# A running sum as one scan instruction, and half of a product moved from GpSimd to VectorE, in a two-layer hybrid decoder

## The chip, the cores and the metric

The kernel runs on one core of a Trainium2 chip. The metric is the device time of one execution in microseconds (us). A run with a profile is one execution on the chip with the hardware profiler on; it has its own time, and the span that its records cover is a little shorter. The engines are PE (TensorE), DVE (VectorE), ACT (ScalarE), POOL (GpSimd) and SP, which only issues DMAs here. Each engine takes its instructions in the order in which the program lists them for that engine.

## The reference

Two decoder layers on 256 positions of width 2048 in float32. In each layer one input projection gives the columns of three token mixers: a gated short convolution, a latent attention of 8 heads, and an RWKV-7 time mixing of 8 heads of 64. Their gated outputs are joined, projected and normed into the residual stream. The change lies in the RWKV branch:

```python
w = -jax.nn.softplus(-(w0 + jnp.tanh(wd) @ w2)) - 0.5
decay = jnp.exp(-jnp.exp(w.astype(jnp.float32)))
a = jax.nn.sigmoid(a0 + ad @ a2)
kk = kk / jnp.maximum(jnp.linalg.norm(kk, axis=-1, keepdims=True), 1e-12)
k = k * (1 + (a - 1) * k_a)
...
def step(state, inp):
    r_t, w_t, k_t, v_t, a_t, b_t = inp          # a_t = -kk, b_t = kk * a
    sa = jnp.einsum('bhvk,bhk->bhv', state, a_t)
    state = (state * w_t[:, :, None, :] + sa[..., None] * b_t[:, :, None, :]
             + v_t[..., None] * k_t[:, :, None, :])
    return state, jnp.einsum('bhvk,bhk->bhv', state, r_t)
...
y = (yf - ym) * lax.rsqrt(yv + RWKV_GN_EPS)     # per head, over 64 channels
```

`decay` is exp(-c * sigmoid(...)) with a constant c, so a product of decays over positions is the exponential of a running sum of sigmoids.

## The kernel before, in words

Channels lie on the 128 partitions and positions along the free axis, so a group of 512 columns is four blocks `b` of 128 channels x 256 positions. Each float32 matmul is three passes (`mm3`, lines 338 to 340): weights and activations are split into a high part `hi_...` (a cast by ACT) and a low rest `lo_...` (a subtraction by DVE), and high x high, high x low and low x high are added in PSUM. A weight tile of two rows of 128 gives a block of 24 matmuls of 128x256; a group of columns has eight such blocks, named here k0+0, k0+2, k4+0 and so on to k12+2.

The order of the work. Each layer goes through the groups k, r, a, v, cq, cc, ch, cb, cg of the input projection (`in_group`), then the key/value projection of the attention (`mla_kv`: four pairs of tiles `pkn` and `pvt`), its query projection (`mla_q`: four of `pqn` and `pqp`), the late groups rg, mg0, mg1, and the output projection. The three mixers are Python generators. After each block of matmuls a `tick` lets every generator run up to its next `yield`, so a yield sets between which blocks a generator's instructions are emitted: one yield fewer, and all that follows in that generator is emitted one tick sooner. A scheduler then merges what was emitted into the order of each engine, with raised priority for weight splits (`split_w`) and for evictions of PSUM.

The RWKV generator (`rwkv`) runs these steps, which the prediction names by their tiles:

- `rwkv_decay`: two low-rank matmuls per block; ACT's Tanh makes the decay's input (`cuma`) and the input of a (`tha`). Six shifted additions on DVE, between the two padded buffers `cuma` and `cumb`, make the running sum within each chunk of 64 positions, with a yield after each. ACT's exponentials of it are `pe` (with minus) and `pinv` (with plus).
- `rwkv_scale`: `kp` is the scaled key, `kkn` the normed key. The tile `bk` holds, for 16 pairs of block and chunk, 64 columns of one of them and 64 of the other, each times `pinv`. Even heads lie on the partitions 0 to 63 and odd heads on 64 to 127; for the odd heads the two are in the other order. The even heads' two products are DVE's, 64 partitions x 1024 each; the odd heads' are POOL's, one per chunk (`chunk`, line 575), eight of 64x256. `ar` holds `kkn` and the receptance times `pe`, eight DVE instructions of 128x256.
- `rwkv_products`: PE's pair products `pg` of `bk` with `ar`, per chunk (line 624).
- `rwkv_inverse`, `rwkv_pairs`: the inverse of a triangular matrix in each chunk, transposes, and products with the values.
- `rwkv_chain`: for the four chunks one after the other, PE's `prh` (state times ar, line 797), DVE's `rhs`, PE's `pu` (line 804), its copies to `uvt` by DVE and ACT, PE's state update `pst` (line 820), and the new state `st` by DVE. After every second chunk PE makes the outputs `py` (lines 773 and 782), and ACT copies them to `y`.
- `rwkv_norm`: the group norm of `y`. DVE's sum `gm`, its scaling, `y` minus `gm`; ACT's square `gsq`; DVE's sum `gv`, an inverse root by twelve small instructions on 128x16 (`grs`, `nr_g`), `y` times `grs`; then PE's transposes `pt` (line 863) and ACT's `yy` from them.
- `rwkv_gate`, after the group rg.

Of the kernel before, what the change touches and what calls it, by code (L numbers as in the profile page):

```python
# [13 lines left out]
AF = mybir.ActivationFunctionType  # L14
ALU = mybir.AluOpType
AX = mybir.AxisListType

P = 128
# [18 lines left out]
KAPPA = float(math.exp(-0.5))  # L37
# [73 lines left out]
def hybrid_layers(ctx: ExitStack, tc: tile.TileContext, x, positions, xT, w_in, w_out, w_uq, w_ukv, par, wa_in, gb_in,  # L111
# [32 lines left out]
    V, A, G, T = Gated(nc.vector, "V"), Gated(nc.scalar, "A"), nc.gpsimd, nc.tensor  # L144

    def after(inst, earlier):

        tc.add_manual_dep(inst.ins, earlier.ins.name,
                          mybir.DependencyInfo(mybir.DependencyClass.NoSync, mybir.DependencyReason.DATA),
                          reason="loads no earlier than needed")  # L150
# [28 lines left out]
    def zeros(rows):  # L179

        return cs[rows, K_CM + P:K_CM + 2 * P].unsqueeze(1).to_broadcast([64, 2, P])
# [3 lines left out]
    def slot(tag, name, shape=(P, 4, S), bufs=1, dt=F32):  # L185
        return sl.tile(list(shape), dt, tag=tag, name=name, bufs=bufs)

    def s4(name, shape=(P, 4, S), dt=F32):
        return slot("s4", name, shape, N4, dt)

    def c4(name, shape=(P, 4, S), dt=F32):
        return slot("c4", name, shape, NC4, dt)

    def s8(name, shape=(P, 8, S), dt=F32):
        return slot("s8", name, shape, N8, dt)
# [154 lines left out]
    def plan():  # L350

        for l in range(L):
            for names in (MAIN, None, LATE):
                if names is None:
                    yield from ((f"ukv{l}_{i}", 0, 2, w_ukv[l, i]) for i in range(4))
                    yield from ((f"uq{l}_{i}", 0, 4, w_uq[l, i]) for i in range(4))
                for name in names or ():
                    first = l == 0 and name == GROUPS[0]
                    for k0, nk in STEPS if first else [(k, 4) for k in (0, 4, 8, 12)]:
                        yield f"{name}{l}", k0, nk, w_in[l, GROUPS.index(name)]  # L360
            for g in range(3):
                yield from ((f"wo{l}_{g}", k0, 4, w_out[l, g]) for k0 in ORDER)
            for i in range(2):
                yield from ((f"wo{l}_3_{i}", k0, 4, w_out[l, 3][:, :, i * 256:i * 256 + 256]) for k0 in ORDER)

    loads, ready, asked = plan(), {}, []
# [62 lines left out]
    def shift_mix(pq, dst, u, mcol):  # L429

        col = pq["col"]
        with tc.high_priority(AHEAD):
            A.activation(dst, u, AF.Identity, scale=col(mcol + pq["om"]))
            V.scalar_tensor_tensor(dst[:, 1:S], u[:, 0:S - 1], col(mcol), dst[:, 1:S], ALU.mult, ALU.add)
# [66 lines left out]
    def rwkv_decay(l, pq, st, us):  # L501
        col = pq["col"]
        wa, ws = c4(f"wa{l}", (P, 2, 512)), c4(f"was{l}", (P, 2, 512), F32R)
        for r in halves:
            after(nc.gpsimd.dma_start(wa[r], wa_in[l].rearrange("(q r) c -> r q c", q=2)), loaded[0])
        A.copy(ws, wa)
        for i in range(2):
            r = halves[1 - i]
            V.tensor_tensor(ws[r, i, :], wa[r, i, :], ws[r, i, :].bitcast(F32), ALU.subtract)
        zl = c4(f"wal{l}", (P, 2, S), F32R)  # L510
        for i, r in enumerate(halves):
            G.tensor_copy(zl[halves[1 - i], i, :].rearrange("p (j c) -> p j c", c=P), zeros(halves[1 - i]))
        wa_x = sm.tile([P, S], F32, tag="rs", name=f"wax{l}", bufs=2)
        shift_mix(pq, wa_x, us, Q_MUWA)
        A.activation(wa_x[0:64, :], wa_x[0:64, :], AF.Tanh)
        cuma = s8(f"cuma{l}", (P, 4, 4, 96))
        cumb = s8(f"cumb{l}", (P, 4, 4, 96))
        V.memset(cuma[:, :, :, 0:32], 0.0)
        V.memset(cumb[:, :, :, 0:32], 0.0)
        tha = s4(f"tha{l}")  # L520
        xh = sm.tile([P, 2, S], F32R, tag="b2", name=f"wah{l}", bufs=3)
        for i, r in enumerate(halves):
            for o in halves:
                A.copy(xh[o, i, :], wa_x[r, :])
            V.tensor_tensor(zl[r, i, :], wa_x[r, :], xh[r, i, :].bitcast(F32), ALU.subtract)

        def lora(o, i, b):
            c = slice(b * P, b * P + P)
            T.matmul(o, ws[:, i, c], xh[:, i, :], start=True, stop=False)
            T.matmul(o, ws[:, i, c], zl[:, i, :], start=False, stop=True)  # L530

        yield
        for b in range(4):
            pw = pm.tile([P, S], F32, tag="m", name=f"pw{l}_{b}")
            lora(pw, 0, b)
            A.activation(cuma[:, b, :, 32:96], pw.rearrange("p (c t) -> p c t", c=4), AF.Tanh,
                         scale=0.5, bias=col(pq["hw"] + b))
            pa = pm.tile([P, S], F32, tag="m", name=f"pa{l}_{b}")
            lora(pa, 1, b)
            A.activation(tha[:, b, :], pa, AF.Tanh, scale=0.5, bias=col(pq["ha"] + b))  # L540
            if b % 2:
                yield
        ca = cuma.rearrange("p b c t -> p (b c) t")
        cb = cumb.rearrange("p b c t -> p (b c) t")
        V.tensor_scalar(ca[:, :, 32:96], ca[:, :, 32:96], 0.5, 0.5, ALU.mult, ALU.add)
        for d in (1, 2, 4, 8, 16, 32):
            V.tensor_tensor(cb[:, :, 32:96], ca[:, :, 32:96], ca[:, :, 32 - d:96 - d], ALU.add)
            ca, cb = cb, ca
            yield
        pe = slot("pe", f"pe{l}", (P, 16, 65))  # L550
        V.memset(pe[:, :, 0:1], 1.0)
        A.activation(pe[:, :, 1:65], ca[:, :, 32:96], AF.Exp, scale=-KAPPA)
        pinv = s4(f"pinv{l}")
        A.activation(pinv.rearrange("p b (c t) -> p (b c) t", t=64), ca[:, :, 32:96], AF.Exp, scale=KAPPA)
        st.update(pe=pe, pinv=pinv, tha=tha)
        yield

    def rwkv_scale(l, pq, st):
        col = pq["col"]
        kx, kkn, rx, tha, pe, pinv = (st[k] for k in ("kx", "kkn", "rx", "tha", "pe", "pinv"))  # L560
        kp = s4(f"kp{l}")
        for b in range(4):
            A.activation(kp[:, b, :], tha[:, b, :], AF.Identity, scale=col(pq["hk"] + b), bias=col(pq["ok"] + b))
        V.tensor_tensor(kp, kp, kx, ALU.mult)
        V.tensor_scalar(tha, tha, 0.5, 0.5, ALU.mult, ALU.add)
        yield
        bk = s8(f"bk{l}", (P, 16, P))
        ar = s8(f"ar{l}", (P, 4, 2, S))
        c16 = lambda a: a.rearrange("p b (c t) -> p (b c) t", t=64)
        lo_, hi_ = halves  # L570
        bkc = bk.rearrange("p (b c) t -> p b c t", c=4)

        def chunk(c, src, at):
            cc = slice(c * 64, c * 64 + 64)
            return G.tensor_tensor(bkc[hi_, :, c, at:at + 64], src[hi_, :, cc], pinv[hi_, :, cc], ALU.mult)

        for c in range(3):
            chunk(c, kp, 0)
        for b in range(4):
            V.scalar_tensor_tensor(chunks(ar[:, b, 0, :]), chunks(kkn[:, b, :]), -1.0,  # L580
                                   pe[:, b * 4:(b + 1) * 4, 0:64], ALU.mult, ALU.mult)
            if b % 2:
                yield
        V.tensor_tensor(kkn, kkn, tha, ALU.mult)
        ready_ = []
        for c in range(4):
            if c == 2:
                chunk(3, kp, 0)
            ready_.append([chunk(c, kkn, 64)])
        yield  # L590
        V.tensor_tensor(bk[lo_, :, 0:64], c16(kkn)[lo_], c16(pinv)[lo_], ALU.mult)
        V.tensor_tensor(bk[lo_, :, 64:128], c16(kp)[lo_], c16(pinv)[lo_], ALU.mult)
        yield
        for b in range(4):
            v = V.tensor_tensor(chunks(ar[:, b, 1, :]), chunks(rx[:, b, :]), pe[:, b * 4:(b + 1) * 4, 1:65], ALU.mult)
        yield
        st["ar"], st["bk"], st["kp"], st["ready"] = ar, bk, kp, [r + [v] for r in ready_]

    def rwkv_v(l, pq, st, uv):
        rx = st["rx"]  # L600
# [734 lines left out]
    for l in range(L):  # L1335
        u, t = {}, {}
# [47 lines left out]
```

## Time and profile before

| | us |
|---|---|
| time of the kernel before, median of 3 runs | 924.45 |
| lowest and highest of them | 924.32, 926.1 |
| the profiled execution | 928.7 |
| span of its records | 926.9 |
| mean granted clock of PE in it | 0.993 |

How to read the rows below. A row of the timeline has the start in us, the duration in us (for several instructions in one row, up to the end of the last), engine, line, operation, what is written `<-` what is read, shapes, and the count. In square brackets stands how long the engine had been idle before it and what ended that. A helper records every operation of DVE and ACT, so their line is L137 throughout and the tile's name tells them apart. A row of the waits has the engine that waited, what it was to do, whose work it waited for, and then the sum, the count and the longest wait in us. A row of the windows has the stretch, its length, the busy time of PE, PE's weight loads, DVE, ACT and POOL with their counts, then the granted clock of PE (1.00 is full), the share of the DMA engines' time and GB/s. A row of the groups has the busy time in us and the mean of one instruction in ns, then the idle time before. A row of the chain has the start, what the piece adds to the chain, and the instruction.

### The profile page before, as it was taken

The page shows a single profiled execution, that of the slowest core. Times are in us where ns is not written, and L with a number is a line of the kernel's source. Part 1 is how long each engine was busy: PE and PEld are TensorE (multiplying, and loading weights), DVE is VectorE, ACT ScalarE, POOL GpSimd, SP SyncE. Part 2 cuts the span into 40 slices and gives each one's busy share as a digit, 9 for nine tenths or more (in the row PEclk, how much of TensorE's full clock was granted, in tenths as well). Part 3 has the DMA queues.
Part 4 walks back from the last instruction along what each step waited for, and adds up shares of the span by engine and source line. Part 5 has one row for each costly group of instructions (what it writes and reads, how often), then busy time and mean ns, then how long its engine had stood idle before and what let it go on. Part 6 is the DMA issues. An engine that isn't in the chain of part 4 may idle for free.

```text
span 926.9 us, 18425 instructions
## 1 busy us (share of the span) xinstructions
PE 909.6 (98%) x7719; PEld 868.5 (94%) x7719; DVE 680.2 (73%) x1132; ACT 466.1 (50%) x716; POOL 44.9 (5%) x59
## 2 busy tenths in 40 slices
PE   8999999999999999999999999999999999999996
PEld 7999999999899999889899999899998999998895
DVE  6687899886479885666767688688865898755665
ACT  5756536443465775434346465364434657654430
POOL 0210120000000000000010003200000000000000
PEclk9999999999999999999999999899999999999998
DMA  8965355354426526955564554354544354359542
GB/s 291 297 197 182 137 189 164 138 183 137 160 96 224 175 99 193 359 177 171 193 211 177 183 182 154 128 180 137 183 139 141 134 204 164 97 182 367 176 135 91
DMA packets 47523, 165.12 MB, mean 178 GB/s; under 512 B 13446, under 2 KB 22198, under 8 KB 32582
## 3 DMA queue, kind: packets, MB, share of 16 engines
q1 hardware_dynamic: 39680, 150.35, 47.4%
q10 hardware_dynamic: 5072, 9.57, 3.4%
q0 software_dynamic: 2688, 4.03, 1.6%
q8 instruction: 60, 0.98, 0.4%
q14 instruction: 23, 0.19, 0.1%
HBM read 158.61 MB, written 5.32 MB: 177 GB/s over the span
## 4 chain that ended last, share of the span: by engine, by line
PE 93%; DVE 3%; DMA 2%; ACT 1%; POOL 1%; SPq 0%; issue 0%; DVEq 0%; ACTq 0%
PE po L338 6%; PE po L340 6%; PE po L339 6%; PE u_mg L340 3%; PE u_mg L338 3%; PE u_mg L339 3%; PE u_ch L338 2%; PE u_cc L338 2%; PE u_cg L340 2%; PE u_cg L339 2%; PE u_cg L338 2%; PE u_rg L340 2%; PE u_cb L340 2%; PE u_cb L339 2%; PE u_cb L338 2%; PE u_a L340 2%
## 5 line engine op out<-in xcount | busy, mean ns | idle before, releaser
L137 DVE TENSOR_TENSOR lo_wo<-w_wo,hi_wo 128x1024 fp32r<-128x1024 f32 x57 | 69.4, 1223 | 51.6 <-ACT hi_wo L137 50.1
L137 ACT CAST hi_wo<-w_wo 128x1024 fp32r<-128x1024 f32 x57 | 59.8, 1053 | 80.8 <-PE po L340 55.7
L338 PE MATMUL u_mg<-x,hi_mg 128*128 128x256 f32 x256 | 72.6, 283 | 0.0
L340 PE MATMUL u_mg<-x,lo_mg 128*128 128x256 f32 x256 | 72.6, 283 | 0.0
L339 PE MATMUL u_mg<-x,hi_mg 128*128 128x256 f32 x256 | 72.6, 283 | 0.0
L137 DVE TENSOR_TENSOR lo_mg<-w_mg,hi_mg 128x1024 fp32r<-128x1024 f32 x32 | 39.0, 1222 | 19.0 <-ACT hi_mg L137 18.9
L340 PEld LDWEIGHTS u_mg<-x,lo_mg 128*128 128x128 f32 x256 | 49.1, 192 | 0.0
L339 PEld LDWEIGHTS u_mg<-x,hi_mg 128*128 128x128 f32 x256 | 49.1, 192 | 0.0
L338 PEld LDWEIGHTS u_mg<-x,hi_mg 128*128 128x128 f32 x256 | 49.0, 192 | 0.0
L137 ACT CAST hi_mg<-w_mg 128x1024 fp32r<-128x1024 f32 x32 | 33.6, 1049 | 25.9 <-PE u_mg L339 18.5
L339 PE MATMUL po<-lo_wo,ma 128*128 128x512 f32 (+1 forms) x128 | 46.4, 362 | 0.0
L340 PE MATMUL po<-hi_wo,ma 128*128 128x512 f32 (+1 forms) x128 | 46.4, 362 | 0.0
L338 PE MATMUL po<-hi_wo,ma 128*128 128x512 f32 (+1 forms) x128 | 45.8, 363 | 0.0
L338 PE MATMUL u_cq<-x,hi_cq 128*128 128x256 f32 x128 | 37.7, 294 | 0.0
L338 PE MATMUL u_k<-x,hi_k 128*128 128x256 f32 x128 | 36.4, 289 | 1.2 <-ACT hi_k L137 1.2
L339 PE MATMUL u_cq<-x,hi_cq 128*128 128x256 f32 x128 | 37.1, 290 | 0.0
L340 PE MATMUL u_cq<-x,lo_cq 128*128 128x256 f32 x128 | 37.1, 290 | 0.0
L338 PE MATMUL u_ch<-x,hi_ch 128*128 128x256 f32 x128 | 37.0, 289 | 0.0
L338 PE MATMUL u_cc<-x,hi_cc 128*128 128x256 f32 x128 | 36.7, 289 | 0.0
L340 PE MATMUL u_cg<-x,lo_cg 128*128 128x256 f32 x128 | 36.6, 286 | 0.0
L338 PE MATMUL u_cg<-x,hi_cg 128*128 128x256 f32 x128 | 36.4, 284 | 0.0
L339 PE MATMUL u_cg<-x,hi_cg 128*128 128x256 f32 x128 | 36.4, 284 | 0.0
(424 smaller groups left out, 3418.4 us busy)
## 6 DMA issues: line engine op xcount, KB each, us to landing
w_wo<-in_w_out_dram SPq DMA_DIRECT2D x24, 1024.0 KB, 6.2
w_mg<-in_w_in_dram SPq DMA_DIRECT2D x16, 1024.0 KB, 4.9
w_r<-in_w_in_dram SPq DMA_DIRECT2D x8, 1024.0 KB, 5.8
w_a<-in_w_in_dram SPq DMA_DIRECT2D x8, 1024.0 KB, 4.8
w_v<-in_w_in_dram SPq DMA_DIRECT2D x8, 1024.0 KB, 4.8
w_cq<-in_w_in_dram SPq DMA_DIRECT2D x8, 1024.0 KB, 4.8
w_cc<-in_w_in_dram SPq DMA_DIRECT2D x8, 1024.0 KB, 4.8
w_ch<-in_w_in_dram SPq DMA_DIRECT2D x8, 1024.0 KB, 5.0
```

The lines of the kernel that those rows point to most:

```text
L137: inst = call(*args, **kwargs)
L338: m = T.matmul(o, lh, rh, start=first, stop=False, skip_group_check=True)
L339: T.matmul(o, lh, rl, start=False, stop=False, skip_group_check=True)
L340: T.matmul(o, ll, rh, start=False, stop=last, skip_group_check=True)
```

## The change

In `rwkv_decay` the two padded buffers become one unpadded `sig`, and a constant `keep` that is 0 at the first position of every chunk and 1 elsewhere, written by POOL. One scan, state = keep x state + sig along all 1024 elements, makes the running sum `cum` in place of six additions. Five of the six yields between the additions go with them. In `rwkv_scale` the odd heads' half of `bk` is written by two DVE products of 64x1024, and POOL's eight products of 64x256 are gone; the first matmul of each chunk's `pg` no longer names POOL's products among those that it comes after.

```diff
-        cuma = s8(f"cuma{l}", (P, 4, 4, 96))
-        cumb = s8(f"cumb{l}", (P, 4, 4, 96))
-        V.memset(cuma[:, :, :, 0:32], 0.0)
-        V.memset(cumb[:, :, :, 0:32], 0.0)
+        sig = s8(f"sig{l}", (P, 16, 64))
+        cum = s8(f"cum{l}", (P, 2, 16, 64))
+        cum, keep = cum[:, 0], cum[:, 1]
+        G.memset(keep, 1.0)
+        G.memset(keep[:, :, 0:1], 0.0)
...
-        V.tensor_scalar(ca[:, :, 32:96], ca[:, :, 32:96], 0.5, 0.5, ALU.mult, ALU.add)
-        for d in (1, 2, 4, 8, 16, 32):
-            V.tensor_tensor(cb[:, :, 32:96], ca[:, :, 32:96], ca[:, :, 32 - d:96 - d], ALU.add)
-            ca, cb = cb, ca
-            yield
+        V.tensor_scalar(sig, sig, 0.5, 0.5, ALU.mult, ALU.add)
+        flat = lambda a: a.rearrange("p c t -> p (c t)")
+        V.tensor_tensor_scan(flat(cum), flat(keep), flat(sig), 0.0, ALU.mult, ALU.add)
+        yield
...
-        for c in range(3):
-            chunk(c, kp, 0)
+        V.tensor_tensor(bk[hi_, :, 0:64], c16(kp)[hi_], c16(pinv)[hi_], ALU.mult)
...
-        ready_ = []
-        for c in range(4):
-            if c == 2:
-                chunk(3, kp, 0)
-            ready_.append([chunk(c, kkn, 64)])
+        V.tensor_tensor(bk[hi_, :, 64:128], c16(kkn)[hi_], c16(pinv)[hi_], ALU.mult)
```

What it does to the order of the instructions, at three places; both layers have the same.

PE's row around the first pair products, in the group cq of the input projection. Before (`x_3` and `cq_12` are its last quarter; `pg_0_1` and `pg_0_0` are chunk 0 for the odd and the even heads):

```order
L339 MATMUL u_cq_1_1254<-x_3_85,hi_cq_12_0_1395 128x256
L340 MATMUL u_cq_1_1254<-x_3_85,lo_cq_12_0_1396 128x256
L624 MATMUL pg_0_1_1494<-ar_1321,bk_1320 128x128 x4
L338 MATMUL u_cq_0_1253<-x_3_85,hi_cq_12_2_1399 128x256
L339 MATMUL u_cq_0_1253<-x_3_85,hi_cq_12_2_1399 128x256
```

After (`x_2` and `cq_8` are the third quarter):

```order
L338 MATMUL u_cq_1_1267<-x_2_84,hi_cq_8_0_1346 128x256
L339 MATMUL u_cq_1_1267<-x_2_84,hi_cq_8_0_1346 128x256
L611 MATMUL pg_0_1_1333<-ar_1198,bk_1197 128x128 x4
L340 MATMUL u_cq_1_1267<-x_2_84,lo_cq_8_0_1347 128x256
L338 MATMUL u_cq_1_1267<-x_2_84,hi_cq_8_0_1346 128x256
```

The pair products moved from behind seven whole blocks of cq to behind four blocks and eight matmuls of the fifth.

PE's row from the end of the key/value projection on. Before, the chain's last steps stand among the query projection's matmuls (`pqn`, `pqp`), and the transposes `pt` inside the group rg, ahead of the attention's first scores `sc_0`:

```order
L340 MATMUL pvt_3_3257<-hi_ukv_3_0_0_3209,hkv_1653 128x256
L797 MATMUL prh_3_3004<-st_2_2971,ar_1321 64x64 x8
L338 MATMUL pqn_0_3307<-hq_1782,hi_uq_0_0_0_3248 128x256
...
L804 MATMUL pu_3_3039<-rhs_3_3013,xq_2415 64x64 x8
L338 MATMUL pqp_0_3308<-hq_1782,hi_uq_0_0_0_3248 128x256
...
L339 MATMUL u_rg_0_3529<-x_3_85,hi_rg_12_2_3749 128x256
L863 MATMUL pt_0_3287<-cs,y_2677 128x128 x4
L863 MATMUL pt_1_3353<-cs,y_2677 128x128 x4
L1041 MATMUL sc_0_3609<-kn_3103,qn_3295 128x128
```

After:

```order
L340 MATMUL pvt_3_3263<-hi_ukv_3_0_0_3216,hkv_1700 128x256
L784 MATMUL prh_3_2847<-st_2_2820,ar_1198 64x64 x8
L791 MATMUL pu_3_2892<-rhs_3_2856,xq_2277 64x64 x8
L760 MATMUL py_1_0_2927<-uvt_1785,gs_1_1331 64x64 x8
...
L769 MATMUL py_1_1_2928<-st_1_2696,ar_1198 64x64
L769 MATMUL py_1_1_2928<-st_2_2820,ar_1198 64x64
L850 MATMUL pt_0_3098<-cs,y_2526 128x128 x4
L850 MATMUL pt_1_3106<-cs,y_2526 128x128 x4
L338 MATMUL pqn_0_3304<-hq_1885,hi_uq_0_0_0_3254 128x256
L339 MATMUL pqn_0_3304<-lq_1886,hi_uq_0_0_0_3254 128x256
```

The chain's last steps and the transposes moved together, ahead of all of the query projection.

DVE's row at the group norm. Before, its instructions have weight splits (`lo_uq`, later `lo_rg`) and rotary products (`qp`, `rt_q`) between them:

```order
L137 TENSOR_REDUCE gm_3142<-y_2677 128x16
L137 TENSOR_TENSOR lo_uq_3_0_0_3420<-w_uq_3_0_3417,hi_uq_3_0_0_3419 128x2x384
L137 TENSOR_SCALAR gm_3142<-gm_3142 128x16
L137 TENSOR_TENSOR qp_3296<-pqp_1_3372,cosT 128x256
L137 TENSOR_TENSOR rt_q_1_3410<-pqp_1_3372,sinT 32x256 x4
L137 TENSOR_TENSOR y_2677<-y_2677,gm_3142 128x1024
```

After:

```order
L137 TENSOR_TENSOR lo_uq_1_0_2_3301<-w_uq_1_0_3294,hi_uq_1_0_2_3300 128x2x384
L137 COPY uvt_1785<-pu_3_2892 64x4x64
L137 TENSOR_TENSOR mc_3211<-cy_2419,mc_3211 128x512 x2
L137 TENSOR_REDUCE gm_2997<-y_2526 128x16
L137 TENSOR_SCALAR gm_2997<-gm_2997 128x16
L137 TENSOR_TENSOR y_2526<-y_2526,gm_2997 128x1024
L137 TENSOR_REDUCE gv_3027<-gsq_3001 128x16
L137 TENSOR_SCALAR gv_3027<-gv_3027 128x16
...
L137 TENSOR_TENSOR y_2526<-y_2526,grs_3029 128x1024
L137 TENSOR_TENSOR yy_3097<-yy_3097,bon_1571 128x512 x2
L137 TENSOR_TENSOR lo_uq_2_0_0_3353<-w_uq_2_0_3350,hi_uq_2_0_0_3352 128x2x384
```

The norm's instructions moved into one piece, ahead of the splits of the third quarter of the query weights. On ACT the copies of the value projection (`vt` from `pvt_0` to `pvt_3`) moved from beside it to behind the first `yy`.

More of the change, by code (lines that the diff above doesn't have):

```diff
@@ L535, in rwkv_decay @@
             lora(pw, 0, b)
-            A.activation(cuma[:, b, :, 32:96], pw.rearrange("p (c t) -> p c t", c=4), AF.Tanh,
+            A.activation(sig[:, 4 * b:4 * b + 4, :], pw.rearrange("p (c t) -> p c t", c=4), AF.Tanh,
                          scale=0.5, bias=col(pq["hw"] + b))
@@ L542, in rwkv_decay @@
                 yield
-        ca = cuma.rearrange("p b c t -> p (b c) t")
-        cb = cumb.rearrange("p b c t -> p (b c) t")
-        V.tensor_scalar(ca[:, :, 32:96], ca[:, :, 32:96], 0.5, 0.5, ALU.mult, ALU.add)
-        for d in (1, 2, 4, 8, 16, 32):
-            V.tensor_tensor(cb[:, :, 32:96], ca[:, :, 32:96], ca[:, :, 32 - d:96 - d], ALU.add)
-            ca, cb = cb, ca
-            yield
+        V.tensor_scalar(sig, sig, 0.5, 0.5, ALU.mult, ALU.add)
+        flat = lambda a: a.rearrange("p c t -> p (c t)")
+        V.tensor_tensor_scan(flat(cum), flat(keep), flat(sig), 0.0, ALU.mult, ALU.add)
+        yield
         pe = slot("pe", f"pe{l}", (P, 16, 65))
         V.memset(pe[:, :, 0:1], 1.0)
-        A.activation(pe[:, :, 1:65], ca[:, :, 32:96], AF.Exp, scale=-KAPPA)
+        A.activation(pe[:, :, 1:65], cum, AF.Exp, scale=-KAPPA)
         pinv = s4(f"pinv{l}")
-        A.activation(pinv.rearrange("p b (c t) -> p (b c) t", t=64), ca[:, :, 32:96], AF.Exp, scale=KAPPA)
+        A.activation(pinv.rearrange("p b (c t) -> p (b c) t", t=64), cum, AF.Exp, scale=KAPPA)
         st.update(pe=pe, pinv=pinv, tha=tha)
@@ L570, in rwkv_scale @@
         lo_, hi_ = halves
[L571 to L575, printed above, removed]
-        for c in range(3):
-            chunk(c, kp, 0)
+        V.tensor_tensor(bk[hi_, :, 0:64], c16(kp)[hi_], c16(pinv)[hi_], ALU.mult)
         for b in range(4):
@@ L596, in rwkv_scale @@
         yield
-        st["ar"], st["bk"], st["kp"], st["ready"] = ar, bk, kp, [r + [v] for r in ready_]
+        st["ar"], st["bk"], st["kp"], st["ready"] = ar, bk, kp, [[v] for _ in range(4)]
     def rwkv_v(l, pq, st, uv):
```

## The prediction

> **What bounds the kernel now.** I read the page first (busy time, chain), then PE's waits, then PE's timeline at the two longest of them, then the rows of DVE, ACT and POOL that the change touches.
>
> ```profile
> PE 909.6 (98%) x7719; PEld 868.5 (94%) x7719; DVE 680.2 (73%) x1132; ACT 466.1 (50%) x716; POOL 44.9 (5%) x59
> PE 93%; DVE 3%; DMA 2%; ACT 1%; POOL 1%; SPq 0%; issue 0%; DVEq 0%; ACTq 0%
> PE pst L820 <- ACT uvt L137: 2.6, 2, 1.3
> PE pg L624 <- POOL bk L575: 1.5, 1, 1.5
> ```
>
> PE is busy for 98% of the span and makes 93% of the chain; PE's matmuls aren't changed. So work saved on DVE or POOL is worth only the waits of PE that it ends (the two listed, 1.3 us per layer and 1.5 once), and work moved in front of PE costs in full. The wait at pg was dearer than it looks:
>
> ```profile
> 582.13 1.16 PE L624 MATMUL pg<-ar,bk 64*128 64x128 f32 x8 [1.46 <-POOL bk L575]
> 583.00:584.00 1.00, 1.00 (x6) 0.80 (x4) 0.68 (x2) 0.00 (x0) 1.00 (x2) 0.62 0.63 246
> 587.00:588.00 1.00, 1.00 (x6) 1.00 (x6) 0.28 (x1) 0.00 (x0) 0.00 (x0) 0.50 0.00 0
> 590.00:591.00 1.00, 1.00 (x11) 0.87 (x12) 0.00 (x0) 1.00 (x3) 0.00 (x0) 0.96 0.00 0
> 248.30 0.69 PE L820 MATMUL pst<-uvt,bkt 128*64 128x64 f32 x16 [1.31 <-ACT uvt L137]
> 103.08 1.06 ACT L137 ACTIVATE pe<-cuma 128x1024 f32<-128x1024 f32 x1 [0.88 <-DVE cuma L137]
> 559.48 1.06 ACT L137 ACTIVATE pe<-cuma 128x1024 f32<-128x1024 f32 x1 [0.89 <-DVE cuma L137]
> 304.33 0.28 PE L1047 MATMUL sc<-kh,q 128*128 128x256 f32 x1
> 765.29 0.28 PE L1047 MATMUL sc<-kh,q 128*128 128x256 f32 x1
> ```
>
> After PE stood for 1.46 us at pg in layer 2, the granted clock (third column from the end in the windows) was 0.62, then 0.50, and 0.96 again in 590 to 591: 583.2 to 590.1, about 6.9 us at half speed. Layer 2 runs 456.40 us behind layer 1 up to the decay (559.48 - 103.08) and 460.96 behind it at the attention's scores (765.29 - 304.33). The 4.56 us between are the wait and the clock: 4.56 - 1.46 = 3.1 us for the clock. The 1.31 us wait at pst left the clock alone.
>
> The profiled execution took 928.7 us, 926.9 of it span. The median of the runs shown is 924.45: 4.25 less, about that loss, so I take it that runs without a profile mostly lack it.
>
> **The change part by part.** First the decay up to the pair products pg.
>
> ```profile
> 90.93 0.69 DVE L137 TENSOR_SCALAR cuma<-cuma 128x1024 f32<-128x1024 f32 x1
> 91.65 1.23 DVE L137 TENSOR_TENSOR cumb<-cuma 128x1024 f32<-128x1024 f32 x1
> 92.51 1.05 ACT L137 CAST hi_v<-w_v 128x1024 fp32r<-128x1024 f32 x1 [1.29 <-PE u_v L339]
> 124.20 1.16 PE L624 MATMUL pg<-ar,bk 64*128 64x128 f32 x8
> 105.00 1.08 ACT L137 ACTIVATE kp<-tha,pc 128x256 f32<-128x256 f32 x2
> 116.86 1.21 DVE L137 TENSOR_TENSOR bk<-kp,pinv 64x1024 f32<-64x1024 f32 x1
> 118.00 1.21 DVE L137 TENSOR_TENSOR kkn<-kkn,tha 128x1024 f32<-128x1024 f32 x1
> L137 DVE TENSOR_TENSOR ar<-rx,pe 128x256 f32<-128x256 f32 x4 | 3.1, 818 | 0.0
> 119.29 6.91 POOL L575 TENSOR_TENSOR bk<-kkn,pinv 64x256 f32<-64x256 f32 x4 [5.23 <-DVE kkn L137]
> 575.68 8.46 POOL L575 TENSOR_TENSOR bk<-kkn,pinv 64x256 f32<-64x256 f32 x4 [5.24 <-DVE kkn L137]
> 263.98 0.12 PE pqp L339
> ```
>
> Six additions of 1.23 us become one scan. No row shows a scan; by the nearest, an elementwise product of as many elements, it takes 1.23 us, and two such, 2.5, bound it above. I take 1.23, because it reads and writes as many elements; below 0.7, the tensor_scalar's row of the same size, it can't be. The Trainium skill ("DVE: opcode table, instruction layouts, handler registers and perf-mode slots", section 6) says that the scan's program runs at half throughput; by that it would be an estimated 2.4 us, and no run so far shows it. Either way it costs nothing here: it starts at 91.6 and ends by 94.1 at the latest, and ACT, which needs it for pe, is casting hi_v until 93.56. So pe starts at 93.6 to 94.1 and not at 103.08.
>
> The removed yields matter more. Five of the decay's ten yields are gone, so every later RWKV step is emitted five ticks sooner, and the orders of the engines change with it. PE's pg stood after seven blocks of u_cq (24 matmuls, 2.88 us at 0.12 us each); now it stands eight matmuls into the fifth. That is three blocks less eight matmuls, 7.7 us, sooner: 124.2 - 7.7 = 116.5 us is when PE asks.
>
> Is DVE ready? pe and pinv of 1.06 and four kp activations (1.08 a pair) hold ACT until 93.6 + 4.3 = 97.9. From there DVE has, ahead of pg, kp, kkn, four bk products (two of them POOL's of before) and five lo_cq: eleven instructions at the pitch of 1.14 (116.86 to 118.00), tha's 0.6, and eight ar: 12.5 + 0.6 + 8 x 0.41 = 16.4 us, so it is done at 114.3, 2.2 us ahead of PE. The 0.41 is the 128x256 row quoted below (rhs); if ar kept 0.82, the mean beside POOL's work above, it would be 117.6, a microsecond late. POOL no longer works there, so I take 0.41. The wait on POOL at pg is gone with POOL: minus 4.56 us against the profiled execution, nothing against most runs. Taking POOL's eight chunk products away frees no engine that anyone else waits for.
>
> Now the other end of the branch. In the order of before, PE's chain steps prh_3, pu_3 and py_1 each have twelve or more of the q projection's matmuls in between, and the transposes pt stand 280 rows later, inside the gate group. In the order of after (the part on the change shows both), prh_3, pu_3, py_1, pt_0 and pt_1 follow each other directly, ahead of the first matmul of the q projection. PE takes its matmuls in order, so it has to stand through the whole group norm. Its rows in before, where it was spread out under other work:
>
> ```profile
> 255.80 0.96 DVE L137 TENSOR_TENSOR lo_uq<-w_uq,hi_uq 128x768 fp32r<-128x768 f32 x1 [1.03 <-ACT hi_uq L137]
> 259.44 0.41 DVE L137 TENSOR_TENSOR rhs<-prh,qs 128x256 f32<-128x256 f32 x1
> 263.00 0.42 DVE L137 COPY uvt<-pu 64x256 f32<-64x256 f32 x1 [2.21 <-PE pu L804]
> 263.45 0.37 ACT L137 COPY uvt<-pu 64x256 f32<-64x256 f32 x1 [2.83 <-DVE uvt L137]
> 266.02 1.08 PE py L773 x32
> 267.10 0.62 PE py L782 x32
> 268.80 0.65 ACT L137 COPY y<-py 128x256 f32<-128x256 f32 x2
> 270.10 1.21 DVE L137 TENSOR_REDUCE gm<-y 128x16 f32<-128x1024 f32 x1
> 274.48 1.23 DVE L137 TENSOR_TENSOR y<-y,gm 128x1024 f32<-128x1024 f32 x1
> 275.80 1.06 ACT L137 ACTIVATE gsq<-y 128x1024 f32<-128x1024 f32 x1 [1.89 <-DVE y L137]
> 280.27 1.22 DVE L137 TENSOR_REDUCE gv<-gsq 128x16 f32<-128x1024 f32 x1
> 298.27 0.17 DVE L137 SCALAR_TENSOR_TENSOR nr_g<-nr_g,gv 128x16 f32<-128x16 f32 x1
> 298.48 0.18 DVE L137 SCALAR_TENSOR_TENSOR grs<-nr_g,grs 128x16 f32<-128x16 f32 x1
> 298.69 1.23 DVE L137 TENSOR_TENSOR y<-y,grs 128x1024 f32<-128x1024 f32 x1
> 302.25 1.93 ACT L137 ACTIVATE yy<-pt,pars 128x256 f32<-128x256 f32 x4 [1.55 <-PE pt L863]
> ```
>
> From the end of py: y copies 0.65, gm 1.21, its scaling 0.2, y minus gm 1.23, the square 1.06, gv 1.22, twelve small operations at the pitch of 0.21 (298.27 to 298.48), 2.5, y times grs 1.23: 9.3 us, in which PE has nothing ahead of pt. In front of it come three shorter waits: pu_3 for rhs, behind vs of the value projection's last tile (0.6); py_1 for uvt, behind lo_uq of 0.96 (0.42 and 0.37 in turn after it: 1.2); prh_2 for st, which now has a lo_uq between its two halves (0.5). Behind it pqn_0 needs the PSUM bank of pvt_0, whose copy by ACT now stands behind the first yy (0.48) and takes about as long as the other copies: 0.6 beyond the transposes. Sum 9.3 + 2.3 + 0.6 = 12.2 us a layer.
>
> What goes: the 1.31 us at pst, since 34 matmuls (4 us) of the key projection now lie between pu_1 and pst_1. That leaves 10.9. Then the clock: a standstill of 9 us after which PE resumes with a dense stream. 1.46 us cost 3.1 us above, so I take 3.1, with bounds 1.7 (a phase half as long as the 6.9 us) and 3.5 (all 6.9 at half speed). The Trainium skill ("TensorE: Matmul & The Clock Gate", Part 1) has the clock fall after an idle window of about 3.4 us and return after a busy one; by that the cost would be an estimated 1.7 and the sum 2.8 us less in all, but the row shows the fall after 1.46 us and 6.9 us at half. I go by the row: 14.0 us per layer, 28.0 for both.
>
> **Sum.** 928.7 - 4.56 + 28.0 = 952.1 us against the profiled execution; against the median, 924.45 + 28.0 = 952.5. I say 952.
>
> **Rivals.** *Faster (the other side).* The place is pt in PE's row: if the norm is over when PE arrives, only the gains are left, two waits of 1.31 at pst and the loss at pg: 928.7 - 4.56 - 2.6 = 921.5. It decides from the point where norm and projection overlap again, a standstill at pt of under 1.3 us. For it: DVE and ACT have idle time (73% and 50%). Against it: the 9.3 us are a chain of dependent operations of which each row has its duration, and no engine is asked for anything else in it.
>
> *A second standstill, at pg.* If the scan is slow or ar stays at 0.82, VectorE, which now makes all of bk, comes a microsecond after PE's 116.5, and each layer pays 1 us and 3.1 for the clock: 952 + 8 = 960. For it: only 2.2 us of slack, and POOL's share has moved onto the engine with 73%. Against: POOL, beside which ar took twice its time, is quiet. A scan as slow as the six additions, 7.4 us (the change not doing what it says), ends at 99.0 and makes pe 5.4 late, 3.2 more than the slack: 952 + 2 x (3.2 + 3.1) = 965.
>
> *Less of a loss.* The clock stays up, or pieces of the norm run ahead: 924.45 + 2 x 8 = 940 at the lowest with 3 us less of the chain and no loss of clock.
>
> **How the numbers follow.** Forecast 0.80; second standstill 0.12 (0.02 of it the slow scan); less of a loss 0.05; faster 0.03. The forecast's own range: the clock's 1.7 to 3.5 and 1.5 us either way for the small waits per layer, 2 x (9.4 + 1.7) to 2 x (12.4 + 3.5), 946 to 956. To leave out no more than 2 in 10 I reach up to the pg case and some way down: 943 to 960. A measurement tells 0.2% (1.8 us) from no change: faster 0.03, same 0.01, slower 0.96.
>
> **What would show it.** In the profile after: PE's largest wait is pt, for DVE's y, twice at 9 us or more, and in each a dip of the granted clock to 0.50 for 3 to 7 us right after; the rows gm to y times grs stand back to back just ahead of pt; no bk row on POOL, no wait of pg for POOL; pe starts at about 94. Wrong would be: no wait at pt, or one below 6 us; a wait at pg for DVE; a scan of over 2.5 us; a layer offset unlike the first layer's loss.

## The result, and the profile after

The changed kernel took 949.26 us (median of 4 runs, 948.5 to 949.95), the kernel before 924.38 (4 runs, 922.16 to 926.1): a ratio of 1.0267, 95% interval 1.0252 to 1.0282. The profiled execution took 948.5 us, its span is 946.7 and the mean granted clock 0.985.

First the page of the changed kernel, busy time and chain, and PE's waits at the steps of the RWKV branch (waits elsewhere, of 2.0 us and less each, are left out):

```profile
PE 911.6 (96%) x7719; PEld 871.0 (92%) x7719; DVE 672.9 (71%) x1122; ACT 467.7 (49%) x716; POOL 22.8 (2%) x47
PE 88%; DVE 4%; DMA 4%; ACT 2%; issue 1%; SPq 0%; DVEq 0%; ACTq 0%
...
PE pt L850 <- DVE y L137: 20.1, 2, 10.1
...
PE pu L791 <- DVE rhs L137: 1.3, 2, 0.6
...
PE py L760 <- DVE uvt L137: 0.6, 2, 0.3
PE prh L784 <- DVE st L137: 0.5, 2, 0.3
```

PE is busy for about as long as before (911.6 against 909.6 us), but its share of the span fell from 98% to 96%: it stands. One wait is new and large, at the transposes pt for DVE's y, 10.1 us in each layer. The waits at pst and at pg are gone from the list. DVE has less to do than before (672.9 against 680.2), so the kernel became slower while the engine that got more products became less busy.

PE's timeline of the changed kernel there, in layer 1, with some rows left out (`...`); the bracket at the end is the time that PE had stood:

```profile
256.80 0.68 PE L784 MATMUL prh<-st,ar 64*64 64x64 f32 x16
258.12 0.68 PE L791 MATMUL pu<-rhs,xq 64*64 64x64 f32 x16 [0.64 <-DVE rhs L137]
...
259.38 0.69 PE L760 MATMUL py<-uvt,gs 128*64 128x64 f32 x16 [0.32 <-DVE uvt L137]
...
261.09 0.68 PE L769 MATMUL py<-st,ar 64*64 64x64 f32 x22
271.84 1.94 PE L850 MATMUL pt<-cs,y 128*128 128x128 f32 x8 [10.07 <-DVE y L137]
273.85 0.58 PE L338 MATMUL pqn<-hq,hi_uq 128*128 128x256 f32 x1
```

And DVE's timeline in the same 10 us:

```profile
261.85 1.29 DVE L137 TENSOR_TENSOR mc<-cy,mc 128x512 fp32r<-128x512 f32 x2 [2.52 <-ACT mc L137]
263.06 1.21 DVE L137 TENSOR_REDUCE gm<-y 128x16 f32<-128x1024 f32 x1
...
264.51 1.23 DVE L137 TENSOR_TENSOR y<-y,gm 128x1024 f32<-128x1024 f32 x1
266.92 1.22 DVE L137 TENSOR_REDUCE gv<-gsq 128x16 f32<-128x1024 f32 x1 [1.18 <-ACT gsq L137]
268.18 0.17 DVE L137 TENSOR_SCALAR gv<-gv 128x16 f32<-128x16 f32 x1
...
270.26 0.17 DVE L137 SCALAR_TENSOR_TENSOR grs<-nr_g,grs 128x16 f32<-128x16 f32 x1
270.47 1.22 DVE L137 TENSOR_TENSOR y<-y,grs 128x1024 f32<-128x1024 f32 x1
```

The norm that took from 270 to 300 us in the trace of before, spread out under PE's matmuls, now runs in one piece of 8.6 us, and PE's pt begins when it ends. Some windows around it, and the two in layer 2 in which the clock changes, with the granted clock third from the end:

```profile
262.00:263.00 1.00, 0.00 (x0) 0.00 (x0) 1.00 (x2) 0.98 (x3) 0.00 (x0) 1.00 0.93 393
263.00:264.00 1.00, 0.00 (x0) 0.00 (x0) 1.00 (x2) 0.01 (x1) 0.40 (x1) 0.88 0.09 33
...
270.00:271.00 1.00, 0.00 (x0) 0.00 (x0) 0.90 (x4) 0.00 (x0) 0.00 (x0) 0.50 0.00 0
...
276.00:277.00 1.00, 1.00 (x6) 1.00 (x6) 0.69 (x1) 0.00 (x0) 0.00 (x0) 0.50 0.00 0
277.00:278.00 1.00, 1.00 (x8) 1.00 (x8) 0.00 (x0) 0.00 (x0) 0.00 (x0) 0.79 0.00 0
278.00:279.00 1.00, 1.00 (x11) 1.00 (x10) 0.00 (x0) 0.43 (x1) 0.00 (x0) 1.00 0.00 0
...
734.00:735.00 1.00, 0.00 (x0) 0.00 (x0) 0.53 (x1) 0.38 (x1) 0.00 (x0) 0.90 0.00 0
745.00:746.00 1.00, 1.00 (x10) 1.00 (x10) 0.51 (x1) 0.00 (x0) 0.00 (x0) 0.98 0.00 0
```

The clock falls within 2 us of PE's last matmul and comes back 5.6 us after PE resumed, at about 277.4. PE's loss by it in layer 1 is 0.16 x 0.5 + 5 x 0.5 + 0.21 = 2.8 us; the same sum over the windows of layer 2, from 740.63 to 745.04, gives 2.2.

The decay and the pair products of the changed kernel, from DVE's, ACT's and PE's timelines and, for ar, the groups:

```profile
91.46 2.29 DVE L137 TENSOR_TENSOR_SCAN cum<-cum,sig 128x1024 f32<-128x1024 f32 x1
93.78 1.07 ACT L137 ACTIVATE pe<-cum 128x1024 f32<-128x1024 f32 x1 [0.48 <-DVE cum L137]
111.64 2.47 DVE L137 TENSOR_TENSOR bk<-kkn,pinv 64x1024 f32<-64x1024 f32 x2
116.26 1.16 PE L611 MATMUL pg<-ar,bk 64*128 64x128 f32 x8
L137 DVE TENSOR_TENSOR ar<-rx,pe 128x256 f32<-128x256 f32 x8 | 2.8, 409 | 0.0
```

The scan takes 2.29 us where an addition took 1.23, pe starts at 93.78, bk ends at 114.11, and PE asks for it at 116.26.

### The profile page after: what moved, and what is told of

It is laid out like the page before. It is cut to its first block, busy times and chain, and to the rows that moved or that the text cites. A ratio compares the mean times of both kernels' runs of the same rounds, so it can differ in the third digit from the quotient of the medians.

```text
span 946.7 us, 18384 instructions
## 1 busy us (share of the span) xinstructions
PE 911.6 (96%) x7719; PEld 871.0 (92%) x7719; DVE 672.9 (71%) x1122; ACT 467.7 (49%) x716; POOL 22.8 (2%) x47
## 4 chain that ended last, share of the span: by engine, by line
PE 88%; DVE 4%; DMA 4%; ACT 2%; issue 1%; SPq 0%; DVEq 0%; ACTq 0%
PE po L338 5%; PE po L340 5%; PE po L339 5%; PE u_mg L340 3%; PE u_mg L339 3%; PE u_mg L338 3%; PE u_cc L338 2%; PE u_cg L340 2%; DMA w_k<-in_w_in_dram 2%; PE u_cq L340 2%; PE u_cg L338 2%; PE u_rg L340 2%; PE u_cb L340 2%; PE u_cb L338 2%; PE u_ch L340 2%; PE u_ch L339 2%
## 5 line engine op out<-in xcount | busy, mean ns | idle before, releaser
L338 PE MATMUL u_k<-x,hi_k 128*128 128x256 f32 x128 | 36.5, 290 | 0.6 <-ACT hi_k L137 0.6
L339 PE MATMUL u_k<-x,hi_k 128*128 128x256 f32 x128 | 36.6, 289 | 0.0
L338 PE MATMUL u_rg<-x,hi_rg 128*128 128x256 f32 x128 | 36.5, 285 | 0.0
L338 PE MATMUL u_cg<-x,hi_cg 128*128 128x256 f32 x128 | 36.4, 284 | 0.0
L340 PE MATMUL u_k<-x,lo_k 128*128 128x256 f32 x128 | 35.9, 287 | 0.5 <-DVE lo_k L137 0.5
L340 PE MATMUL u_rg<-x,lo_rg 128*128 128x256 f32 x128 | 36.2, 283 | 0.0
L338 PE MATMUL u_a<-x,hi_a 128*128 128x256 f32 x128 | 36.2, 283 | 0.0
```

What stands on the lines that cost most here:

```text
L338: m = T.matmul(o, lh, rh, start=first, stop=False, skip_group_check=True)
L339: T.matmul(o, lh, rl, start=False, stop=False, skip_group_check=True)
L340: T.matmul(o, ll, rh, start=False, stop=last, skip_group_check=True)
```

## The experiments

Ten kernels were run, in three groups, each group on one chip beside its own runs of the kernel before. Ratios stand against the before of the group. The changed kernel had a group of its own; the medians of before are 924.38 there, 924.54 for the first four, 925.05 for the next four and 926.99 for the last two, so a difference of a microsecond between groups says nothing.

**1. The changed kernel with its five yields put back** (12 runs).

```diff
         V.tensor_tensor_scan(flat(cum), flat(keep), flat(sig), 0.0, ALU.mult, ALU.add)
         yield
+        for _ in range(5):
+            yield
```

> The changed kernel with five yields put back behind the scan; scan and VectorE's products stay. Theory (the loss is PE standing for the group norm, because the missing yields pull the transposes ahead of the query projection): PE's row has the chain's tail again as before the change, no wait at pt, no dip of the clock there, both waits of 1.3 us at pst are back; 922 to 925 us, no change against before beyond 0.2%. Rival (the added work on VectorE, a scan of 2.29 us and two more products of 1.2, holds PE up): still above 940.

Measured: 921.84 us (921.21 to 922.18), ratio 0.9961, 0.9945 to 0.9977. All that the change computes is there, and the loss is gone. PE's longest wait in it is again the one at pst, with no wait at pt:

```profile
PE pst L809 <- ACT uvt L137: 2.6, 2, 1.3
```

So the rival that blames the work on VectorE falls. The kernel is even 2.7 us below before, just outside what I expected; the section on what was not expected comes back to it.

**2. VectorE's products alone, in the kernel before** (12 runs). Additions and yields as before.

```diff
-        for c in range(3):
-            chunk(c, kp, 0)
+        V.tensor_tensor(bk[hi_, :, 0:64], c16(kp)[hi_], c16(pinv)[hi_], ALU.mult)
...
-            ready_.append([chunk(c, kkn, 64)])
+        V.tensor_tensor(bk[hi_, :, 64:128], c16(kkn)[hi_], c16(pinv)[hi_], ALU.mult)
```

> Before, with only the odd heads' products moved from POOL to VectorE; six additions and all yields stay. Theory: 922 to 925, the only gain that a wait of pg for POOL can no longer happen (it cost one profiled execution 4.6 us). Rival (more work on VectorE): slower, by up to the 2 x 2 x 1.2 = 5 us of the added products.

Measured: 922.86 us (922.07 to 924.56), ratio 0.9975, 0.9951 to 0.9999. The four more products of 1.2 us on VectorE cost nothing that shows; PE's list of waits has no pg in it. The order didn't stay quite the same, though: the scheduler put the first pg behind 192 matmuls of cq in place of 168.

**3. The changed kernel with yields further down** (12 runs).

```diff
                 V.tensor_tensor(rhs, pr_, qs[:, c], ALU.add)
                 yield
+                if c in (2, 3):
+                    yield
...
                     moved.append(A.copy(dst, pu[rs[par]]))
             yield
+            if c in (2, 3):
+                yield
...
                 state = new
             yield
+            if c in (2,):
+                yield
```

> The changed kernel with five yields added later, in the chain's chunks 2 and 3 (one behind each rhs, each copy of uvt, and the state update of chunk 2). Theory: pg stays early as in the changed kernel, pst_1 keeps its 34 matmuls in between, and prh_3, pu_3, py_1 and pt stand among the query projection's matmuls and in the gate group again; so neither the wait at pt nor those at pst: 924.4 - 2.6 = 921.8, range 920 to 923. Rival (VectorE's work): above 940.

Measured: 921.21 us (918.72 to 924.17), ratio 0.9951, 0.9933 to 0.9970; the profiled execution took 919.27, span 917.5. Neither pt nor pst is in PE's list of waits:

```profile
PE pzero L243 <- DVE zeror L137: 2.0, 1, 2.0
PE cwt L1206 <- DVE cw L137: 1.4, 1, 1.4
PE xt L1227 <- DVE xr L137: 0.8, 1, 0.8
PE prh L784 <- DVE st L137: 0.5, 2, 0.3
```

It is faster than before beyond its interval, at the time that was expected. Against the first kernel, which still has the waits at pst, its fastest run is 2.5 us lower and its median 0.6: it spreads over 5.5 us, and the gain of 2.6 is seen in part of its runs only.

**4. The kernel before with one yield moved** (12 runs).

```diff
             ca, cb = cb, ca
-            yield
+            if d < 32:
+                yield
...
                     moved.append(A.copy(dst, pu[rs[par]]))
             yield
+            if c == 1:
+                yield
```

> Before, with one yield taken out behind the sixth addition and one put in behind the uvt copies of chunk 1; additions and POOL's products stay. Theory: the waits of 1.3 us at pst go as in the changed kernel, without any of the change: 924.4 - 2.6 = 921.8, range 920 to 924 (the wait of pg for POOL may fall on some runs). Rival (the gains need the scan): 924.

Measured: 928.71 us (926.26 to 931.83), ratio 1.0040, 1.0022 to 1.0058: slower, and both expectations missed. The waits at pst did go, but PE now waits for POOL at pg in both layers. In layer 1 PE asks for it only 0.2 us sooner than in before (124.02 against 124.20); what moved is DVE's `kkn`, which POOL's last four products need. It starts at 119.46 in place of 118.00, so POOL starts them at 120.74 in place of 119.29. PE's rows at pg, and windows of 2 us behind each:

```profile
125.85 1.38 PE L625 MATMUL pg<-ar,bk 64*128 64x128 f32 x8 [1.82 <-POOL bk L576]
126.00:128.00 2.00, 2.00 (x12) 1.78 (x13) 0.69 (x1) 0.01 (x1) 1.86 (x3) 0.66 0.89 266
128.00:130.00 2.00, 2.00 (x11) 2.00 (x11) 0.94 (x1) 1.03 (x1) 0.00 (x0) 0.50 0.68 283
584.33 1.16 PE L625 MATMUL pg<-ar,bk 64*128 64x128 f32 x8 [1.82 <-POOL bk L576]
584.00:586.00 2.00, 1.67 (x13) 1.55 (x13) 0.48 (x1) 0.05 (x1) 2.00 (x4) 1.00 0.81 221
586.00:588.00 2.00, 2.00 (x18) 1.87 (x17) 1.18 (x2) 1.00 (x1) 0.35 (x1) 1.00 0.89 373
```

The same wait of 1.82 us brought the clock to 0.50 in one layer (0.68 + 1.0 = 1.7 us lost in these two windows) and left it at 1.00 in the other. So a wait of this size has no fixed price; the last section comes back to it.

**5. The kernel before without the five yields** (4 runs).

```diff
             V.tensor_tensor(cb[:, :, 32:96], ca[:, :, 32:96], ca[:, :, 32 - d:96 - d], ALU.add)
             ca, cb = cb, ca
-            yield
+        yield
```

> Before, with the five yields between the additions taken out and nothing else changed: six additions, POOL's products. PE's row from the end of the key/value projection is that of the changed kernel, transposes ahead of the query projection. Theory: PE stands about 10 us at pt in each layer, with the dip of the clock: 949, range 945 to 953. Rival (VectorE's scan and products): 924.

Measured: 959.1 us (957.02 to 959.26), ratio 1.0358, 1.0335 to 1.0382. This is the mirror of the first: nothing of the change is in it but the order, and the stand at pt is there at the same length, with waits for POOL added:

```profile
PE pt L863 <- DVE y L137: 20.2, 2, 10.1
PE pg L624 <- POOL bk L575: 2.3, 2, 1.1
```

The time is above the range that I gave, 10.8 us above the changed kernel's profiled execution. The trace accounts for it to within a microsecond: 2.3 us of waits at pg; 1.0 more at the start, at u_k (1.6 against 0.6); 3.8 of clock, which was at 0.50 for two more stretches of 3.41 us, from 11.7 and from 127.7; and 4.5 in pg itself, whose pieces in PE's row add up to 7.85 us a layer (one of 2.05 and five of 1.16) against 5.59 in the changed kernel (the last section says why a piece's length depends on its place). The order alone makes the loss of the changed kernel; with POOL's products left in place it cost more.

**6. PE kept busy during the norm** (4 runs). The changed kernel with 76 matmuls on constants ahead of the transposes, whose results the transposes overwrite.

```diff
             pt = pm.tile([P, 2, S], F32, tag="m", name=f"pt{l}_{b2}")
+            for i in range(0 if b2 else 76):
+                m = T.matmul(pt[:, 0, :], ones[:, 0:P], ones, start=True, stop=True)
+                if i == 0:
+                    after(m, st["py"])
```

> The changed kernel with 76 matmuls of 128x256 on constants (9.1 us at 0.12) between py_1 and pt, into the tile that the transposes then overwrite; their result isn't used. The order is otherwise the same. Theory: the wait at pt falls to about 1 us, the norm takes as long as it did, the clock stays at 1.00, so only the loss of the clock goes: 949.3 - (2.7 + 2.2) = 944.4, range 943 to 946. Rival (the clock is most of the loss): below 935. Rival (the clock costs nothing): 949.

Measured: 945.43 us (944.98 to 948.86), ratio 1.0224, 1.0197 to 1.0251. The norm is as long as it was and the clock stays up, by PE's timeline and the window from its resuming on:

```profile
262.18 9.38 PE L849 MATMUL pt<-ones 128*128 128x256 f32 x76
272.24 1.09 PE L855 MATMUL pt<-cs,y 128*128 128x128 f32 x8 [0.68 <-DVE y L137]
273.82 0.39 PE L338 MATMUL pqn<-hq,hi_uq 128*128 128x256 f32 x1 [0.48 <-ACT vt L137]
274.00:278.00 4.00, 4.00 (x35) 4.00 (x36) 1.41 (x3) 2.80 (x7) 0.00 (x0) 1.00 0.00 0
```

The gain is 949.26 - 945.43 = 3.8 us, or 4.0 by the ratios ((1.0267 - 1.0224) x 924.4). The clock's loss of 5.0 went, and 2 x 0.5 came back: at full clock PE is early at pqn_0, whose PSUM bank waits for ACT's vt. That wait was hidden in the slow transposes of the changed kernel. The clock is some 4 to 5 us of the loss, the stand itself 20.

**7. Only the transposes moved back** (4 runs).

```diff
+        for _ in range(2):
+            yield
         yy = s4(f"yy{l}")
```

> The changed kernel with two yields ahead of the transposes: pt now stands behind the 46 first matmuls of the query projection, prh_3, pu_3 and py_1 stay together. Theory with the PSUM bank: pqn_0 still needs the bank of pvt_0, whose copy by ACT stands behind the square of the norm, so PE stands about 5.5 us at pqn_0 in place of 10 at pt, with a dip of the clock of 2 to 3 us: 924.4 + 2 x (5.5 + 1.2 - 1.3 + 2.5) = 940, range 936 to 943. Rival (the transposes alone hold PE): the 46 matmuls (5.5 us) fill the wait, a wait of 4.5 at pt remains, and none at pqn: 934 to 938.

Measured: 939.09 us (938.17 to 939.98), ratio 1.0147, 1.0121 to 1.0173. PE's and ACT's timelines:

```profile
268.72 0.58 PE L338 MATMUL pqn<-hq,hi_uq 128*128 128x256 f32 x1 [5.43 <-ACT vt L137]
...
275.78 1.04 PE L852 MATMUL pt<-cs,y 128*128 128x128 f32 x8
267.35 1.06 ACT L137 ACTIVATE gsq<-y 128x1024 f32<-128x1024 f32 x1 [2.82 <-DVE y L137]
268.31 1.18 ACT L137 COPY vt<-pvt 128x256 f32<-128x256 f32 x4
```

The wait moved from pt to pqn_0: ACT, in its own order, copies vt and so frees the bank only after the square of the norm. With the transposes out of the way PE still stands 5.43 us, for a copy that has nothing to do with the norm. Theory and size were right; the rival without the bank has its wait in the wrong place.

**8. The scan and the order without VectorE's products** (4 runs). The changed kernel's decay with `rwkv_scale` of before, so the second kernel's edit the other way round:

```diff
-        V.tensor_tensor(bk[hi_, :, 0:64], c16(kp)[hi_], c16(pinv)[hi_], ALU.mult)
+        for c in range(3):
+            chunk(c, kp, 0)
...
-        V.tensor_tensor(bk[hi_, :, 64:128], c16(kkn)[hi_], c16(pinv)[hi_], ALU.mult)
+            ready_.append([chunk(c, kkn, 64)])
```

> The changed kernel with POOL's eight products as before: the scan and the missing yields alone. Theory: the stand at pt as in the changed kernel, and since pg stands 4 us earlier still in PE's row, a wait of pg for POOL or for VectorE's ar in each layer, 3 us or more with a dip of the clock: 955 to 967. Rival (VectorE's two products hold PE up): faster than the changed kernel, 944 to 947.

Measured: 958.43 us (956.86 to 959.96), ratio 1.0356, 1.0332 to 1.0381. PE waits for POOL at pg in each layer, on top of the stand at pt:

```profile
PE pt L861 <- DVE y L137: 20.1, 2, 10.1
PE pg L622 <- POOL bk L573: 6.2, 2, 3.1
```

So the products on VectorE are worth 8 to 9 us once pg stands this early (9.2 by the medians, 958.43 - 949.26, and 8.2 by the ratios, since the two kernels ran in different groups): they are the part of the change that helps.

**9 and 10. Two more ways to place the yields** (12 runs each, in one group). The ninth is the changed kernel with

```diff
         V.tensor_tensor_scan(flat(cum), flat(keep), flat(sig), 0.0, ALU.mult, ALU.add)
         yield
+        for _ in range(4):
+            yield
...
                     moved.append(A.copy(dst, pu[rs[par]]))
             yield
+            if c in (1,):
+                yield
```

The tenth has the second kernel's edit and the fourth's together, so it keeps the six additions:

```diff
+        V.tensor_tensor(bk[hi_, :, 0:64], c16(kp)[hi_], c16(pinv)[hi_], ALU.mult)
...
+            if d < 32:
+                yield
...
+            if c == 1:
+                yield
```

> The changed kernel with four yields put back behind the scan and one behind the uvt copies of the chain's chunk 1: the tail of the chain spread out as with the yields in the chain, pst_1 with 34 matmuls in between, and pg 40 rows (4.8 us) later in PE's row than in the changed kernel. Theory: no wait at pt, pst or pg: the 921.84 of the five yields put back, less 2 x 1.3 = 919.2, range 918 to 921. Whether the spread of the kernel with the yields in the chain (918.72 to 924.17) came of its early pg is asked too: if so, the runs here lie within 1 us of each other; if not, they spread as far.

> Before, with the odd heads' products on VectorE, one yield taken out behind the sixth addition and one put in behind the uvt copies of chunk 1; the six additions stay. Theory (the scan saves nothing that PE waits for; the products take away the wait for POOL, the yield the waits at pst): 919 to 921, as good as the same with the scan. Rival (the scan itself is worth something): slower than the other kernel of this call by more than 1 us.

Measured: 921.44 us (919.51 to 923.19), ratio 0.9943, 0.9919 to 0.9966, with the scan; 922.87 (921.99 to 925.45), ratio 0.9957, 0.9939 to 0.9976, with the additions. Both are faster than before and neither has a wait at pt, pst or pg, as expected, but both times lie above their ranges (918 to 921 and 919 to 921). The two ran side by side, and the tenth is the slower by 1.43 us between the medians: its fastest run, 921.99, lies above the ninth's median. That is more than the 1 us by which the rival, that the scan itself is worth something, was to be known. But PE waits for neither the scan nor the additions. What differs in PE's row is pg, which takes 5.53 us a layer in the ninth (pieces of 1.16, 1.16, 2.05 and 1.16) and 6.41 in the tenth (2.60, 1.16, 1.16 and 1.49): 1.8 us for both layers. So the scan's gain can be placed in the order that comes with it rather than in VectorE's time; that is argued from the rows, and no run separates the two.

The ninth's runs spread over 3.7 us, less than the third's 5.5 but well over the 1 us that was to show that the early pg made the spread. So the early pg isn't the whole of it. The ninth's profiled execution, at its slow end with 923.19, shows another cause far from the change, at the start of the kernel:

```profile
PE u_k L338 <- ACT hi_k L137: 2.8, 1, 2.8
```

ACT's cast of hi_k waits there for the first weights from memory, and behind PE's wait the clock was at 0.50 from 14.8 to 18.2, another 1.7 us. In the profiled execution of the third kernel, at 919.27, the same wait is 0.4 us and the clock stays up. That is 4 us between two executions before the change is reached; whether it makes all of the spread stays open.

## Why the prediction was right

The direction, the place and the mechanism were as predicted, and 949.26 lies 2.7 us below the forecast. That the sum came so near is in part luck, since errors of its terms cancel. Term by term:

- *The stand at pt.* Predicted 9.3 us, measured 10.07 in each layer. The norm's own rows fit (8.6 us from gm to the end of y times grs). The missing 0.8 is in front of it: the copies of y, predicted to start with the end of py, stood behind ACT's casts mc of the convolution, and DVE's gm behind mc at 261.85.
- *The small waits.* Predicted 2.3 us a layer, measured 0.64 + 0.32 + 0.25 = 1.2. The wait of py for uvt was over-sized, 1.2 against 0.32: DVE's copy of uvt started at 258.92, right behind a lo_uq that was already under way when pu ran.
- *pqn_0 for its bank.* Predicted 0.6, measured 0, because the transposes took 1.94 us at half clock. The sixth kernel shows it at 0.48 with the clock up, and the seventh at 5.43 with pt gone.
- *The clock.* Predicted 3.1 us a layer from one row, measured 2.8 and 2.2 by the windows; the sixth kernel got 3.8 of the 5.0 back. The Trainium skill ("TensorE: Matmul & The Clock Gate", Part 1) gives at least one idle window of about 3.4 us before the fall and at least one busy one before the return. Here the clock fell at 263.8, 2.0 us after PE's last matmul at 261.77, sooner than by the page, and in layer 2 at 734.8, 4.2 us after it, within the page's rule; the return took 5.6 and 4.4 us of work, which is within it too. The estimate of 1.7 that the prediction made from the page was too low and my 3.1 too high.
- *The waits that go.* pst as predicted, 2.6 in all. At pg the predicted margin of 2.2 us was 2.15 (114.11 to 116.26), with ar at 409 ns as assumed.
- *The scan.* I took 1.23 us and gave 2.5 as the bound; it is 2.29. The Trainium skill's half throughput ("DVE: opcode table, instruction layouts, handler registers and perf-mode slots", section 6) agrees with the trace, 2.29 against 1.22 for a product of as many elements. The time doesn't depend on it, as the prediction said: pe starts at 93.78, 0.48 us after ACT was free, and the 2.15 us of margin at pg are left.
- *What was missing.* py takes 2.7 us without its wait (258.73 to 261.77, less 0.32), against 1.77 in the third kernel, since its matmuls stand in another order. That is 1.9 us for both layers, not foreseen. So per layer the stand and py were 1.7 us longer than forecast, and the small waits, the bank and the clock 2.3 us shorter: 13.4 where 14.0 was forecast.

Against the profiled execution of the third kernel, which has the same work and no stand, the sum closes: 946.7 - 917.5 = 29.2 us of span, and the terms are 20.1 at pt, 1.9 at pu and py, 1.9 of longer py, and 5.0 of clock, 28.9. (prh waits in both.)

The assumption that runs of before mostly lack the loss at pg holds as far as the clock tells. Of the 35 runs of before in the first group, 28 have a mean granted clock of 0.995 or more and took 922.79 to 926.17 us; the other seven took 925.12 to 934.96 (the profiled execution with the loss shows 0.993). Even so their median, 924.54, lies above the second kernel's 922.86 and the first's 921.84. So the base without the change's order is nearer 922, and the loss by the order nearer 27.4 (949.26 - 921.84, or 28.3 by the ratios) than the 25 of the comparison, where 28.0 was forecast: the forecast's 2.7 us too many lie for the most part in its base.

## What to carry to other kernels

Where the order of an in-order engine follows from where generators yield, taking out instructions together with their yields is two changes, and the second can be the bigger: compare the engine's row before and after, and for each instruction that moved ahead ask what has to be finished before it. An instruction that is needed late shouldn't stand ahead of work that is ready, and nor should an eviction whose bank that work needs. What is gained on engines that aren't the bound shows only as waits that end on the one that is.

## What the runs showed that I had not expected

A wait of PE of 1.82 us lowered the granted clock in one layer and not in the other of the same execution (the fourth kernel); in before, one of 1.46 did and one of 1.31 did not. Part of that can be read from the traces. Within a trace the clock changes only on a fixed grid of 3.41 us: the stretches at 0.50 lasted 3.41 us in the fourth kernel (126.63 to 130.04), 6.83 in before (583.25 to 590.08), 13.65 and 10.24 in the changed kernel, which is one, two, four and three steps, and the last two begin 471.04 us apart, 138 steps of 3.413. The fourth kernel's wait in layer 1 lies whole within one step (123.22 to 126.63); the one in layer 2 falls on a border at 584.01, 1.51 us ahead of it and 0.31 behind. The grid lies differently in each trace: its first border is 0.93 us into the span in the changed kernel and 3.24 in the first experiment. How much idle time within a step is enough is not settled: 1.46 us was in before, 1.31 was not there, and 1.51 was not in the fourth kernel. So a short stand costs between nothing and the 3.1 us of before on top of itself, and kernels with such waits spread: before over 12 us, the first kernel, which has no wait above 1.3 us besides those at the start and the end, over 1 us. The grid's place would explain such a spread, but that was not measured by itself, and the third and the ninth kernel spread by 5.5 and 3.7 us without such waits.

Pair products of the odd and the even heads run side by side where they alternate in PE's row. In the trace of before eight matmuls of one parity (all of odd or all of even heads) take as long as sixteen of both in the first experiment's, where the single records start in pairs 7 ns apart (124.711 and 124.718, then 124.924 and 124.931):

```profile
125.83 1.16 PE L624 MATMUL pg<-ar,bk 64*128 64x128 f32 x8
124.71 1.16 PE L613 MATMUL pg<-ar,bk 64*128 64x128 f32 x16
```

Before has layer 1's pg in five pieces of 6.7 us (four of 1.16 and one of 2.06), the first experiment in four of 5.54. That is 1.2 us a layer, and with it most of the 2.7 us between the two kernels can be placed; the rest would be the waits for POOL in some runs of before. The second kernel fits in between: its pg takes 6.41 us a layer, 0.9 more than the first's, and its median is 1.0 us higher. All of this is argued from rows; no run changed the alternation alone.
